# Down products in another order: high products of four chunks first, the sixth product's last chunks by bank pairs, and four tiles' norms in common stages

## The chip, the cores and the metric

The kernel runs on one core of a Trainium2 chip. The metric is device time in microseconds of one execution; smaller is better. All outputs are float32.

## The reference

One layer of a streaming encoder over 1024 tokens of width 1024: a half feed-forward block (FFN 1), a mixer of two attentions, and a second half feed-forward block (FFN 2). What the change touches is the second matrix product of each feed-forward block and the norm that follows:

```python
def rms_norm(x, g):
    x32 = x.astype(jnp.float32)
    y = x32 * lax.rsqrt(jnp.mean(x32 * x32, axis=-1, keepdims=True) + EPS)
    return (y * g.astype(jnp.float32)).astype(x.dtype)

def swiglu(u, w_gate, w_up, w_down):
    return (jax.nn.silu(u @ w_gate) * (u @ w_up)) @ w_down

def sublayer(h, i, fn, resid_w):
    ...
    u = rms_norm(h, norm_pre[l, i]) * (1.0 + scale) + shift
    return h + resid_w * gate * rms_norm(fn(u), norm_post[l, i])

h = sublayer(h, 0, lambda u: swiglu(u, ffn1_w_gate[l], ffn1_w_up[l], ffn1_w_down[l]), 0.5)
h = sublayer(h, 1, ..., 1.0)
h = sublayer(h, 2, lambda u: swiglu(u, ffn2_w_gate[l], ffn2_w_up[l], ffn2_w_down[l]), 0.5)
```

The product with `w_down` is 1024 tokens by 2816 by 1024.

## The kernel before

**Numbers.** A float32 product is made of three passes. Each operand is split into a high part (a rounded copy, made by ScalarE, `ACT.copy`) and a low part (the rest, made by VectorE, `tensor_sub`); TensorE adds high x high, high x low and low x high. In the down stage one 128 x 512 piece of an operand comes from DRAM into a staging tile `stg`, and `halves` (lines 217 and 218) makes `sbH`, `sbL` (activations, the stationary side) or `tbH`, `tbL` (weights, the moving side) of it.

**Seven products.** Each big matrix product is done by a scheme with seven half-size products in place of eight (Strassen's, in Winograd's form): sums and differences of the quarters of both matrices are made beforehand and lie in DRAM (`hd`, `d_S`, `d_T`). In the down stage (`ffn`, from line 558) the loop over `p` runs the seven products. The first six have 11 chunks `c` of 128 along the inner dimension; a chunk has four token tiles `m` with a PSUM bank each, and three matmuls of 128x128 by 128x512 a bank (`mm`, lines 578 to 582): 132 matmuls a product. Products use bank set A or B in turns; sixth and seventh both use A. The seventh (`p == 6`) goes over the chunks twice, in `h = 0` for banks 0 and 1 and in `h = 1` for banks 2 and 3, with 256 columns of `sb` each time.

**Buffers.** There are six staging tiles (`STG = 6`), that is, three chunks' worth; six buffers each of `sbH` and `sbL` (`SB = 6`), and eleven each of `tbH` and `tbL`. A staging tile is free again when both the cast on ACT and the subtraction on DVE have read it, and only then can the load of a later piece be issued on the queue of the SP engine.

**After a product** VectorE or ScalarE adds or copies the banks into the eight token tiles `y` (lines 643 to 656). The first four tiles are complete after the fifth product (`p == 4`, line 653); the others after the seventh. The sixth product's sums are read out of the banks at line 656 (`y[4 + m] += bank[m]`); the seventh product adds on in the same banks, so its first matmul into a bank waits for that line's read of the bank.

**Norms.** `finish(t)` loads a residual tile (`res`, two buffers in FFN 1, seven in FFN 2), and `post_norm_tile` takes the sum of squares on ACT (`Square` with accumulation), a `Sqrt` on ACT, a reciprocal, a scalar-tensor-tensor and an addition on DVE, and the store. In FFN 1 `pre_norm` follows for the next sublayer: again a square, a root and a reciprocal, and a multiplication (line 164). The norms of the four first tiles are called one after another after the fifth product.

**Order.** Work is written in the order shown; a scheduler places the instructions on each engine's queue, and every queue is then served strictly in its order. The code around the down stage (`hidden` for the last chunk pair, on DVE) directly precedes the first product.

Of the kernel before, what the change touches and what calls it, by code (L numbers as in the profile page):

```python
# [12 lines left out]
F32 = mybir.dt.float32  # L13
F32R = mybir.dt.float32r
BF16 = mybir.dt.bfloat16
AF = mybir.ActivationFunctionType
ALU = mybir.AluOpType
# [3 lines left out]
P = 128  # L21
# [25 lines left out]
def build(ctx, tc, A, out):  # L47
# [148 lines left out]
    def wproj(ps, w, half):  # L196

        H, L = w
        mm3(ps, [((H[:, k * P:(k + 1) * P], L[:, k * P:(k + 1) * P]), U[k, half]) for k in range(NK)])

    def post_norm_tile(y, g, res, dst, parts=1, tail=False):

# [297 lines left out]
    def ffn(wg, wu, wd, start, pending, steps_fn, per_pair, steps2_fn, i, res_src, dst):  # L500
# [57 lines left out]
        open_y()  # L558
        with tc.tile_pool(name="ffb0", bufs=1, side="left", reuse_waits="tile") as np_, \
                tc.tile_pool(name="ffb", bufs=1, side="left", reuse_waits="tile") as fp, \  # L560
                tc.tile_pool(name="ffb_ps", bufs=4, space=PSUM, reuse_waits="tile") as psum:
            grow = np_.tile([P, D], F32, name="grow", tag="grow")
            if i == 2:
# [11 lines left out]
                loads.append(SP.dma_start(t, A[wd][c][:, B[n]] if n in B else hd[n, c]))  # L575
                return t

            def mm(ps, s, t, ts, first, last, check):
                (sH, sL), (tH, tL) = s, t
                PE.matmul(ps, sH[:, ts], tH, start=first, stop=False, skip_group_check=not check)  # L580
                PE.matmul(ps, sH[:, ts], tL, start=False, stop=False, skip_group_check=not check)  # L581
                PE.matmul(ps, sL[:, ts], tH, start=False, stop=last, skip_group_check=not check)  # L582

            copies = []
            y = [y_tile(t) for t in range(NT)]
# [3 lines left out]
            def finish(t):  # L589
# [4 lines left out]
                if i + 1 in ab:  # L594
                    pre_norm(y[t])

            for p, (sn, tn, bk) in enumerate((("A11", "B11", "A"), ("A12", "B21", "B"), ("S2", "T2", "A"), ("S1", "T1", "B"),
                                              ("S4", "B22", "B"), ("S3", "T3", "A"), ("A22", "T4", "A"))):
                if p in (0, 1, 3):
# [3 lines left out]
                bank = banks[bk]  # L603
                fresh = p in (0, 1, 3)
                if p < 6:
                    for c in range(NPAIR):
                        ahead = ExitStack()
                        if p == 4 and c >= 3:

                            for ins in copies:  # L610
                                ahead.enter_context(tc.issue_after(ins))
                        with ahead:
                            s, t = halves(fp, raw(sn, c), "sb", SB), halves(fp, raw(tn, c), "tb", NPAIR)
                        if c in STEPS[p]:
                            next(steps, None)
                        for m in range(4):
                            mm(bank[m], s, t, slice(m * P, (m + 1) * P), fresh and c == 0, c == NPAIR - 1, fresh)
                else:
                    ts = []
                    turned = iter(())  # L620
# [2 lines left out]
                    for h in range(2):  # L623
                        for c in range(NPAIR):
                            if h == 0 and c == 0:
                                next(steps, None)
                            with ExitStack() as ahead:
                                if h == 0 and c >= 3:
                                    for ins in copies:
                                        ahead.enter_context(tc.issue_after(ins))  # L630
                                r = raw(sn, c)
                                s = halves(fp, r[:, h * 256:(h + 1) * 256], "sb", SB, 256)
                                if h == 0:
                                    ts.append(halves(fp, raw(tn, c), "tb", NPAIR))
# [8 lines left out]
                for m in range(4):  # L643
# [7 lines left out]
                        copies.append((V.tensor_copy if m % 2 else ACT.copy)(y[4 + m][:, d1], bank[m]).ins)  # L651
                    elif p == 4:
                        V.tensor_add(y[m][:, d1], bank[m], y[m][:, d1])
                        finish(m)
                    elif p == 5:
                        copies.append(V.tensor_add(y[4 + m][:, d1], bank[m], y[4 + m][:, d1]).ins)  # L656
                if p == 6:
# [739 lines left out]
```

## Time and profile before

| | us |
|---|---|
| median of 3 runs (2235.43 to 2240.99) | 2236.72 |
| profiled execution | 2242.12 |
| its span, first to last instruction | 2240.4 |
| DVE busy | 1552.1 |
| ACT busy | 1050.0 |
| down stage of FFN 1, first matmul | 486.87 |
| fifth product of FFN 1 ends about | 642.8 |
| down stage of FFN 2, first matmul | 2013.84 |
| last matmul of FFN 2 about | 2228.9 |

The profile's page gives the engines' busy time and the groups of instructions; the trace behind it gives every instruction's start, the idle time before it in brackets with what ended it, and windows in which busy time, instruction count and the granted clock of TensorE are summed. PE is TensorE, DVE is VectorE, ACT is ScalarE, SPq is the queue on which DMAs are issued. A matmul's shown length is longer than the distance to the next one, since matmuls are pipelined.

### The profile page before, as it was taken

How to read it: one execution, taken by the hardware profiler on the slowest of the kernel's cores; microseconds unless marked ns; L12 is line 12 of the kernel's file. 1: busy time of each engine (PE TensorE's matmuls, PEld its weight loads, DVE VectorE, ACT ScalarE, POOL GpSimd, SP SyncE). 2: the span in 40 equal slices, each digit the busy share in tenths (PEclk: the TensorE clock that was granted, in tenths of full speed). 3: DMA queues.
4: the chain of work that ended last, by engine and by line, in shares of the span. 5: the costliest groups of instructions: out<-in, count | busy, mean ns of one | idle time of the engine just before them, and what ended most of it. 6: DMA issues, size and time to landing. Idle time of an engine off the chain costs nothing.

```text
span 2240.4 us, 28449 instructions
## 1 busy us (share of the span) xinstructions
PE 2155.7 (96%) x10328; PEld 1780.0 (79%) x10328; DVE 1552.1 (69%) x2646; ACT 1050.0 (47%) x1893; POOL 61.5 (3%) x84
## 2 busy tenths in 40 slices
PE   6999999999998999999999999999999999999997
PEld 4777788878887877888888988788877788878886
DVE  7979767567577688576677676665985766655566
ACT  6633324235456556455455454565733333334454
POOL 0000000000000011001011000000000000000000
PEclk9999999999999999999999999999999999999999
DMA  8488635359785111110211123653474544538666
GB/s 327 146 281 280 211 130 185 127 183 328 245 291 201 50 45 46 33 54 26 70 55 64 36 94 100 236 202 128 148 239 166 184 173 144 179 111 277 215 224 213
DMA packets 139792, 361.27 MB, mean 161 GB/s; under 512 B 19458, under 2 KB 23682, under 8 KB 139651
## 3 DMA queue, kind: packets, MB, share of 16 engines
q1 hardware_dynamic: 138018, 353.68, 46.4%
q0 software_dynamic: 1632, 5.77, 0.7%
q8 instruction: 81, 1.33, 0.2%
q14 instruction: 61, 0.49, 0.1%
HBM read 270.77 MB, written 88.62 MB: 160 GB/s over the span
## 4 chain that ended last, share of the span: by engine, by line
PE 68%; DVE 19%; DMA 6%; ACT 4%; issue 3%; SPq 0%; DVEq 0%; ACTq 0%
PE bank L295 8%; PE bank L293 7%; PE bank L294 7%; PE pps L841 4%; PE pps L843 4%; PE pps L845 4%; PE bankA L581 3%; PE bankA L582 3%; PE bankA L580 3%; PE bankB L580 3%; PE bankB L582 3%; PE bankB L581 3%; DVE f L1050 2%; DVE wsL L218 2%; DMA wada<-in_wada 2%
## 5 line engine op out<-in xcount | busy, mean ns | idle before, releaser
L841 PE MATMUL pps<-uH,wsH 128*128 128x512 f32 x512 | 209.0, 408 | 0.0
L843 PE MATMUL pps<-uL,wsH 128*128 128x512 f32 x512 | 203.8, 398 | 0.0
L845 PE MATMUL pps<-uH,wsL 128*128 128x512 f32 x512 | 203.2, 397 | 0.0
L218 DVE TENSOR_TENSOR tbL<-stg,tbH 128x512 fp32r<-128x512 f32 x154 | 105.9, 689 | 97.9 <-ACT tbH L217 97.6
L217 ACT CAST tbH<-stg 128x512 fp32r<-128x512 f32 x154 | 95.6, 621 | 141.9 <-DMA stg<-d_T 98.8
L581 PE MATMUL bankA<-tbL,sbH 128*128 128x512 f32 x352 | 139.8, 397 | 6.3 <-DVE tbL L218 6.3
L580 PE MATMUL bankA<-tbH,sbH 128*128 128x512 f32 x352 | 140.1, 398 | 5.5 <-DVE y L656 5.1
L293 PE MATMUL bank<-uH,wsH 128*128 128x512 f32 x352 | 139.1, 401 | 4.1 <-ACT wsH L217 3.5
L294 PE MATMUL bank<-uL,wsH 128*128 128x512 f32 x352 | 140.2, 398 | 1.6 <-DVE uL L748 1.5
L582 PE MATMUL bankA<-tbH,sbL 128*128 128x512 f32 x352 | 139.6, 396 | 0.7 <-DVE sbL L218 0.7
L295 PE MATMUL bank<-uH,wsL 128*128 128x512 f32 x352 | 139.5, 397 | 0.6 <-DVE wsL L218 0.6
L134 DVE TENSOR_TENSOR wsL<-raw,wsH 128x1024 fp32r<-128x1024 f32 x72 | 88.0, 1222 | 68.1 <-ACT wsH L133 67.6
L217 ACT CAST wsH<-s 128x1024 fp32r<-128x1024 f32 x88 | 92.2, 1049 | 85.8 <-DVE s L327 69.8
L217 ACT CAST sbH<-stg 128x512 fp32r<-128x512 f32 (+1 forms) x176 | 98.3, 565 | 62.7 <-DMA stg<-hd_A 47.4
L218 DVE TENSOR_TENSOR sbL<-stg,sbH 128x512 fp32r<-128x512 f32 (+1 forms) x176 | 108.5, 620 | 27.0 <-ACT sbH L217 26.1
L360 ACT COPY q<-bank 128x512 f32<-128x512 f32 x44 | 25.5, 588 | 193.1 <-PE bank L295 193.1
L845 PEld LDWEIGHTS pps<-uH,wsL 128*128 128x128 f32 x512 | 96.6, 189 | 17.7
L218 DVE TENSOR_TENSOR wsL<-s,wsH 128x1024 fp32r<-128x1024 f32 x88 | 107.0, 1217 | 3.5 <-ACT wsH L217 3.2
L841 PEld LDWEIGHTS pps<-uH,wsH 128*128 128x128 f32 x512 | 97.3, 190 | 14.5
L843 PEld LDWEIGHTS pps<-uL,wsH 128*128 128x128 f32 x512 | 97.0, 189 | 14.3
L217 ACT CAST wsH<-raw 128x1024 fp32r<-128x1024 f32 (+1 forms) x88 | 73.3, 834 | 74.0 <-PE bank L294 49.8
L580 PE MATMUL bankB<-tbH,sbH 128*128 128x512 f32 x264 | 102.7, 389 | 0.0
(246 smaller groups left out, 5905.7 us busy)
## 6 DMA issues: line engine op xcount, KB each, us to landing
wada<-in_wada SPq DMA_DIRECT2D x56, 512.0 KB, 5.7
raw<-in_wg SPq DMA_DIRECT2D x50, 512.0 KB, 6.5
raw<-in_wu SPq DMA_DIRECT2D x50, 512.0 KB, 4.6
raw<-in_wd SPq DMA_DIRECT2D x44, 512.0 KB, 4.3
stg<-hd_A SPq DMA_DIRECT2D x88, 256.0 KB, 4.5
stg<-d_S SPq DMA_DIRECT2D x88, 256.0 KB, 3.5
stg<-d_T SPq DMA_DIRECT2D x88, 256.0 KB, 3.9
d_S<-s SPq DMA_DIRECT2D x40, 512.0 KB, 2.7
```

The costliest lines, as they stand in the source:

```text
L134: eng.tensor_sub(l, raw, h.bitcast(F32))
L217: ACT.copy(h, src)
L218: eng.tensor_sub(l, src, h.bitcast(F32))
L293: PE.matmul(ps, H[:, ks], bH, start=first and k == 0, stop=False, skip_group_check=not first)
L294: PE.matmul(ps, H[:, ks], bL, start=False, stop=False, skip_group_check=not first)
L295: PE.matmul(ps, L[:, ks], bH, start=False, stop=k == 3, skip_group_check=not first)
L580: PE.matmul(ps, sH[:, ts], tH, start=first, stop=False, skip_group_check=not check)
L581: PE.matmul(ps, sH[:, ts], tL, start=False, stop=False, skip_group_check=not check)
L582: PE.matmul(ps, sL[:, ts], tH, start=False, stop=last, skip_group_check=not check)
L841: PE.matmul(ps, aH, bH, start=i == 0, stop=False)
L843: PE.matmul(ps, aH, bL, start=False, stop=False)
L845: PE.matmul(ps, aL, bH, start=False, stop=i == n - 1)
```

## The change

Three edits, all in the down stage of both feed-forward blocks.

1. In the first product the high x high matmuls of chunks 0 to 3 (16 of them) are issued first, and then the other two passes of the four chunks (32).
2. In the sixth product the last three chunks are done for banks 0 and 1, and then for banks 2 and 3.
3. The norms of the tiles 0 to 3 are no longer four chains. `rstd4` takes the squares of four tiles into four columns, and one root and one reciprocal serve all four; `finish4` does the rest tile by tile. It is a generator that the sixth product advances by one step a chunk, and the seventh too (`due`).

```diff
+    def rstd4(pool, srcs):
+        ss = pool.tile([P, 4], F32, name="ss4", tag="ss4", bufs=2)
+        for n, src in enumerate(srcs):
+            junk = mpool.tile([P, D + 64], BF16, name="junk", tag="junk", bufs=1)
+            ACT.activation(junk[:, :D], src, AF.Square, scale=1.0 / 32.0, accum_out=ss[:, n:n + 1])
+            yield
+        sq = pool.tile([P, 4], F32, name="sq4", tag="sq4", bufs=2)
+        ACT.activation(sq, ss, AF.Sqrt, bias=eps)
+        r = pool.tile([P, 4], F32, name="rs4", tag="rs4", bufs=2)
+        V.reciprocal(r, sq)
+        return r
...
-            def mm(ps, s, t, ts, first, last, check):
+            def mm(ps, s, t, ts, first, last, check, part=(0, 1, 2)):
                 (sH, sL), (tH, tL) = s, t
-                PE.matmul(ps, sH[:, ts], tH, start=first, stop=False, skip_group_check=not check)
-                PE.matmul(ps, sH[:, ts], tL, start=False, stop=False, skip_group_check=not check)
-                PE.matmul(ps, sL[:, ts], tH, start=False, stop=last, skip_group_check=not check)
+                for n, (a, b) in enumerate(((sH, tH), (sH, tL), (sL, tH))):
+                    if n in part:
+                        PE.matmul(ps, a[:, ts], b, start=first and n == 0, stop=last and n == 2, skip_group_check=not check)
...
+            def finish4():
+                r = yield from rstd4(nrm, [y[t] for t in range(4)])
+                yield
+                for t in range(4):
+                    res = np_.tile([P, D], F32, name="res", tag="res", bufs=res_bufs)
+                    SP.dma_start(res, res_src(t))
+                    V.scalar_tensor_tensor(y[t], y[t], r[:, t:t + 1], grow, ALU.mult, ALU.mult)
+                    V.tensor_add(y[t], y[t], res)
+                    SP.dma_start(dst(t), y[t])
+                    yield
+                if i + 1 in ab:
+                    r = yield from rstd4(nrm, [y[t] for t in range(4)])
+                    yield
+                    for t in range(4):
+                        V.tensor_scalar_mul(y[t], y[t], r[:, t:t + 1])
+                        yield
...
-                        for m in range(4):
-                            mm(bank[m], s, t, slice(m * P, (m + 1) * P), fresh and c == 0, c == NPAIR - 1, fresh)
+                        if p == 5:
+                            next(due, None)
+
+                        def block(c, s, t, ms=range(4), **kw):
+                            for m in ms:
+                                mm(bank[m], s, t, slice(m * P, (m + 1) * P), fresh and c == 0, c == NPAIR - 1, fresh, **kw)
+
+                        if p == 0 and c < 4:
+                            block(c, s, t, part=(0,))
+                            held.append((c, s, t))
+                            if c == 3:
+                                for x in held:
+                                    block(*x, part=(1, 2))
+                        elif p == 5 and c >= NPAIR - 3:
+                            block(c, s, t, (0, 1))
+                            held.append((c, s, t))
+                            if c == NPAIR - 1:
+                                for x in held:
+                                    block(*x, (2, 3))
+                        else:
+                            block(c, s, t)
...
+                            if h == 0:
+                                next(due, None)
+                            else:
+                                for _ in due:
+                                    pass
...
                         V.tensor_add(y[m][:, d1], bank[m], y[m][:, d1])
-                        finish(m)
+                        if m == 3:
+                            due = finish4()
```

**TensorE at the start of FFN 1's down stage.** The names carry buffer numbers: before, chunk 0 has `tbH_3809`, `tbL_3810`, `sbH_3803` and `sbL_3804`; banks are `bankA_3797` to `bankA_3800`. Before:

```order
L295 MATMUL bank_3635<-T4H_723,wsL_3682 128x512
L580 MATMUL bankA_3797<-tbH_3809,sbH_3803 128x512
L581 MATMUL bankA_3797<-tbL_3810,sbH_3803 128x512
L582 MATMUL bankA_3797<-tbH_3809,sbL_3804 128x512
L580 MATMUL bankA_3798<-tbH_3809,sbH_3803 128x512
L581 MATMUL bankA_3798<-tbL_3810,sbH_3803 128x512
```

In the changed kernel (its line 596 is the matmul; chunk 0 has 3806 to 3813, chunk 2 `tbH_3844`, chunk 3 `tbH_3860`; banks 3800 to 3803), from the end of chunk 2's high products on:

```order
L596 MATMUL bankA_3802<-tbH_3844,sbH_3838 128x512
L596 MATMUL bankA_3803<-tbH_3844,sbH_3838 128x512
L596 MATMUL bankA_3800<-tbH_3860,sbH_3854 128x512
L596 MATMUL bankA_3801<-tbH_3860,sbH_3854 128x512
L596 MATMUL bankA_3802<-tbH_3860,sbH_3854 128x512
L596 MATMUL bankA_3803<-tbH_3860,sbH_3854 128x512
L596 MATMUL bankA_3800<-tbL_3813,sbH_3806 128x512
L596 MATMUL bankA_3800<-tbH_3812,sbL_3807 128x512
```

Chunk 3's four high products now stand ahead of every matmul that uses a low part.

**VectorE where FFN 1's sixth product ends.** Before, the last stretch of the four chains of norms (tiles `y0` to `y3`) stands ahead of the four reads of the banks (line 656); `sbL` and `tbL` of size 256 and 512 are operands of the seventh product.

```order
L149 RECIPROCAL rs_5258<-sq_5256 128x1
L149 RECIPROCAL rs_5269<-sq_5267 128x1
L206 SCALAR_TENSOR_TENSOR y3_3792<-y3_3792,rs_5269,grow_3788 128x1024
L164 TENSOR_SCALAR y2_3791<-y2_3791,rs_5258 128x1024
L208 TENSOR_TENSOR y3_3792<-y3_3792,res_5262 128x1024
L656 TENSOR_TENSOR y4_3793<-bankA_3797,y4_3793 128x512
```

In the changed kernel (line 211 is the reciprocal, 619 the addition of the residual, 626 the multiplication, 716 the read of a bank, 231 the subtraction):

```order
L619 TENSOR_TENSOR y2_3794<-y2_3794,res_5408 128x1024
L619 TENSOR_TENSOR y3_3795<-y3_3795,res_5437 128x1024
L231 TENSOR_TENSOR sbL_5516<-stg_5513,sbH_5515 128x256
L231 TENSOR_TENSOR tbL_5522<-stg_5519,tbH_5521 128x512
L231 TENSOR_TENSOR sbL_5536<-stg_5533,sbH_5535 128x256
L211 RECIPROCAL rs4_5553<-sq4_5551 128x4
L626 TENSOR_SCALAR y0_3792<-y0_3792,rs4_5553 128x1024
L626 TENSOR_SCALAR y1_3793<-y1_3793,rs4_5553 128x1024
L626 TENSOR_SCALAR y2_3794<-y2_3794,rs4_5553 128x1024
L716 TENSOR_TENSOR y4_3796<-bankA_3800,y4_3796 128x512
L716 TENSOR_TENSOR y5_3797<-bankA_3801,y5_3797 128x512
L231 TENSOR_TENSOR tbL_5542<-stg_5539,tbH_5541 128x512
```

The reads of banks 0 and 1 now stand behind the second common reciprocal and three multiplications; the reads of banks 2 and 3 stand five rows further down.

More of the change, by code (lines that the diff above doesn't have):

```diff
@@ L560, in ffn @@
                 tc.tile_pool(name="ffb", bufs=1, side="left", reuse_waits="tile") as fp, \
+                tc.tile_pool(name="nrm", bufs=1, side="left", reuse_waits="tile") as nrm, \
                 tc.tile_pool(name="ffb_ps", bufs=4, space=PSUM, reuse_waits="tile") as psum:
@@ L595, in finish @@
                     pre_norm(y[t])
+            def finish4():
[14 more added lines that the diff above has]
+                        yield
+            due = iter(())
             for p, (sn, tn, bk) in enumerate((("A11", "B11", "A"), ("A12", "B21", "B"), ("S2", "T2", "A"), ("S1", "T1", "B"),
@@ L605, in ffn @@
                 if p < 6:
+                    held = []
                     for c in range(NPAIR):
```

## Prediction

> **What bounds the kernel now.** I read the page's busy shares first, then the waits of TensorE over the two down stages (FFN 1 from 478 to 740 us, FFN 2 from 1990 us to the end), then TensorE's windows and the timeline around the two largest waits.
>
> ```profile
> PE 2155.7 (96%) x10328; PEld 1780.0 (79%) x10328; DVE 1552.1 (69%) x2646; ACT 1050.0 (47%) x1893; POOL 61.5 (3%) x84
> PE bankA L580 <- DVE y L656: 5.1, 1, 5.1
> PE bankA L581 <- DVE tbL L218: 3.0, 1, 3.0
> PE bankA L581 <- DVE tbL L218: 3.3, 2, 3.0
> ```
>
> TensorE is the bound. The second and third rows are FFN 1's, the last FFN 2's: two waits of 3.0 us at the start of the first product, one of 5.1 us between sixth and seventh product in FFN 1, and none there in FFN 2. The change touches these places. No instruction of weight is added or taken away, so everything turns on TensorE's idle time and its clock. The windows (time, PE busy and count, granted clock, DMA share, GB/s) price both:
>
> ```profile
> 486.87:496.39 9.52, 6.49 (x16) 0.65 0.77 256
> 2013.84:2023.11 9.27, 6.24 (x21) 0.82 0.75 248
> 672.37:681.38 9.01, 3.88 (x11) 0.81 0.78 263
> 681.38:694.30 12.92, 12.92 (x58) 1.00 0.86 291
> ```
>
> A warm matmul takes 12.92 / 57 gaps = 0.2267 us. The first three windows are the three places; the counts hold one matmul of the product before or of the window's edge. What is lost is the window less its matmuls at 0.2267: 15 of the product's own between 486.87 and 496.43 lose 9.56 - 15 x 0.2267 = 6.16 us; 19 between 2013.84 and 2023.11 lose 9.27 - 4.31 = 4.96 us; ten from 672.37 to 681.38 lose 9.01 - 2.27 = 6.74 us. So each stall costs more than its wait, and the rest is the clock (here each row also has PEld, DVE, ACT and POOL before the clock):
>
> ```profile
> 489.56:492.98 3.42, 2.69 (x6) 2.16 (x7) 3.08 (x6) 0.00 (x0) 0.30 (x1) 0.51 0.99 320
> 492.98:496.39 3.41, 3.41 (x9) 2.65 (x8) 0.85 (x2) 1.25 (x3) 0.00 (x0) 0.50 1.02 338
> 496.39:499.80 3.41, 3.41 (x16) 2.79 (x15) 3.23 (x6) 2.99 (x5) 0.00 (x0) 0.99 1.03 306
> 677.30:680.71 3.41, 2.82 (x7) 2.27 (x8) 3.41 (x8) 1.62 (x4) 0.00 (x0) 0.51 0.81 275
> ```
>
> The clock is granted in steps of 3.41 us. At 0.50 a step has 8 gaps between its 9 matmuls, at 0.99 it has 15 between 16: 47% of a cold step is lost, 1.6 us. A step that was 79% busy (2.69 of 3.42) was followed by a cold one, a step 83% busy (2.82) by a warm one. A restart was cold for 2.9 us at least (677.9 to 680.8) and 6.1 us at most (490.3 to 496.4): 1.36 to 2.88 us.
>
> **Part 1, high products of four chunks first.** FFN 1's timeline:
>
> ```profile
> 484.56 0.61 ACT L217 CAST tbH<-stg 128x512 fp32r<-128x512 f32 x1
> 486.87 0.39 PE L580 MATMUL bankA<-tbH,sbH 128*128 128x512 f32 x1
> 488.94 0.69 DVE L218 TENSOR_TENSOR sbL<-stg,sbH 128x512 fp32r<-128x512 f32 x1
> 489.66 0.33 SPq L575 DMA_DIRECT2D stg<-hd_A  x1
> 490.26 0.33 SPq L575 DMA_DIRECT2D stg<-in_wd  x1
> 490.29 0.80 PE L581 MATMUL bankA<-tbL,sbH 128*128 128x512 f32 x1 [3.03 <-DVE tbL L218]
> 494.89 0.62 ACT L217 CAST sbH<-stg 128x512 fp32r<-128x512 f32 x1 [9.71 <-DMA stg<-hd_A]
> 495.42 0.61 ACT L217 CAST tbH<-stg 128x512 fp32r<-128x512 f32 x1
> ```
>
> TensorE begins at 486.87 and needs the first low part at once; VectorE is still busy with the stage before and makes its first, `sbL`, at 488.94. The 16 high products would be 16 x 0.2267 = 3.6 us of work for a wait of 3.0. But only six staging tiles exist, three chunks' worth: their casts end at 484.56 + 0.61, and then ACT sits idle for 9.71 us. Chunk 3's pieces need tiles that VectorE has first to read: the load is issued at 489.66, 0.03 us after `sbL` is made, and its weights' cast ends at 495.42 + 0.61 = 496.03. In the change chunk 3's four high products stand ahead of all low products in TensorE's queue, so 32 low products whose operands are ready from 490 us on stand behind them. The wait moves from the low part of chunk 0 to the high part of chunk 3. SP's and VectorE's orders at this place are as before, so I take 496.08 for the restart (0.05 us from the cast's end to the matmul), with 12 matmuls done: 9.21 - 12 x 0.2267 = 6.49 us lost, and the cold restart (the idle time fills more than one step) between 1.36 and 2.88; I take the middle, 2.1, since where in a step it restarts is open. 8.6 against 6.16: **+2.4 us** (+1.7 to +3.2).
>
> ```profile
> 2013.84 0.39 PE L580 MATMUL bankA<-tbH,sbH 128*128 128x512 f32 x1
> 2016.63 0.33 SPq L575 DMA_DIRECT2D stg<-hd_A  x1
> 2022.60 0.62 ACT L217 CAST tbH<-stg 128x512 fp32r<-128x512 f32 x1
> ```
>
> FFN 2 is alike: first matmul 2013.84, chunk 3's load issued 2016.63, its weights cast by 2023.22, restart at 2023.26 or 2023.27. 9.42 - 12 x 0.2267 = 6.70 us, and 2.1 for the clock: 8.8 against 4.96, **+3.8 us** (+3.1 to +4.6). Before, TensorE used the gap for chunks 0 and 1 at half clock; in the change it cannot.
>
> The Trainium skill ("TensorE: Matmul & The Clock Gate", "Part 1: The HAM clock gate", under "What's actually happening") says that TensorE falls to half clock after at least one idle window of about 3.4 us, and is at full clock again after one busy one. The trace agrees on the second (492.98 to 496.39 is full, and the next step stands at 0.99) but not on the first: a stall of 3.03 us already made the next step cold. By that page each restart pays one cold window, 1.6 us: the two places would come to +1.9 and +3.3 in place of +2.4 and +3.8, an estimate, and the sum below to 1.0 us less. Its rule speaks against gathering idle time into one gap as well.
>
> **Parts 2 and 3, FFN 1.** The timeline around the wait of 5.1 us:
>
> ```profile
> 645.52 2.48 DVE L653 TENSOR_TENSOR y<-bankB,y 128x512 f32<-128x512 f32 x4
> 646.48 1.05 ACT L143 ACTIVATE junk<-y 128x1024 bf16<-128x1024 f32 x1
> 648.16 1.28 ACT L147 ACT_TABLE_LOAD   x1
> 673.87 0.16 DVE L149 RECIPROCAL rs<-sq 128x1 f32<-128x1 f32 x1 [1.23 <-ACT sq L147]
> 677.07 1.88 DVE L656 TENSOR_TENSOR y<-bankA,y 128x512 f32<-128x512 f32 x3
> 677.89 0.76 PE L580 MATMUL bankA<-tbH,sbH 128*128 128x512 f32 x1 [5.13 <-DVE y L656]
> 679.86 0.68 DVE L218 TENSOR_TENSOR tbL<-stg,tbH 128x512 fp32r<-128x512 f32 x1
> 680.60 0.32 SPq L575 DMA_DIRECT2D stg<-d_T  x1
> 691.85 0.69 DVE L218 TENSOR_TENSOR tbL<-stg,tbH 128x512 fp32r<-128x512 f32 x1 [0.21 <-ACT tbH L217]
> ```
>
> The seventh product's first matmul may only start once VectorE has read the bank at line 656, and that stands behind the fourth chain of norms: the last reciprocal at 673.87 waits for ACT. What the chains cost, by the groups (busy time, mean ns, idle before) and the residual's loads:
>
> ```profile
> L206 DVE SCALAR_TENSOR_TENSOR y<-y,rs,grow 128x1024 f32<-128x1024 f32 (+1 forms) x26 | 31.0, 1200 | 0.6
> L208 DVE TENSOR_TENSOR y<-y,res 128x1024 f32<-128x1024 f32 (+1 forms) x26 | 29.4, 1138 | 0.1
> L164 DVE TENSOR_SCALAR y<-y,rs 128x1024 f32<-128x1024 f32 x20 | 15.4, 768 | 1.6 <-DMA h_dram<-y 1.5
> DMA to landing us min/median/max: 3.9/4.9/6.2
> ```
>
> The change by hand. The sums are ready at 648.0; four squares of 1.05 us between casts, and the table load of 1.28, put the common root at about 654.4. Reciprocal, two scalings and two additions (2 x 1.20 + 2 x 1.14) end at 659.3; two more scalings with the subtractions of chunks 8 to 10 between them at 665.3, in time for the sixth product's last chunk. The residuals of tiles 2 and 3 stand on SP behind the stores of tiles 0 and 1, issued about 660, and land about 4.9 us later, 665 to 666.5; the additions end at 667.7, the second squares and root at 670.0, the reciprocal and three multiplications (0.67 each) at 672.7, and the reads of banks 0 and 1 (0.62 each) at 673.9. TensorE, ready at 672.37 + 0.23 = 672.6, starts about 673.9 in place of 677.9: 4.0 us earlier.
>
> Not all of it is kept. The seventh product's later loads are released by VectorE three chunks back, in a loop that starts with the first low parts after line 656. The change puts a low part between the reads of banks 0, 1 and 2, 3, so line 656's last read ends at about 677.4 by hand, against 679.6 (just ahead of `tbL` at 679.86): the loop moves by 2.2 us. Before, chunk 10's `tbL` ended at 692.54, about 0.6 us before TensorE used it. TensorE can gain 2.2 + 0.6 = **2.8 us**, and I take that; the bounds are 6.7 (the whole loss) and nothing. Bank pairs alone cost nothing: the last 36 matmuls are the same, and VectorE gets banks 0 and 1 earlier than it can use them, behind the norms.
>
> **Parts 2 and 3, FFN 2.**
>
> ```profile
> 2191.13 0.37 SPq L575 DMA_DIRECT2D stg<-d_T  x1
> 2196.50 2.73 DVE L656 TENSOR_TENSOR y<-bankA,y 128x512 f32<-128x512 f32 x4 [0.74 <-PE bankA L582]
> 2212.46 0.69 DVE L218 TENSOR_TENSOR tbL<-stg,tbH 128x512 fp32r<-128x512 f32 x1 [2.11 <-ACT tbH L217]
> 2212.48 0.50 PE L580 MATMUL bankA<-tbH,sbH 128*128 128x512 f32 x1 [0.38 <-ACT tbH L217]
> ```
>
> Here line 656 waits for TensorE and there is no stall to win. The common root makes the stores of tiles 2 and 3 later, and the seventh product's loads of chunks 1 and 2 (2191.13 is the issue of chunk 1's weights) stand on SP behind the last of them, about 2.8 us later than before by a hand sum like the one above. The start at 2198.8 is still met, but chunks 6 to 10, of which chunk 10 already waits 0.38 us, come about 1 us later. I take **+0.3 us**; bounds -0.7 (the small waits gone) and +2.5 (the delay in full). The fewer roots and reciprocals (about 0.3 and 0.16 us each) run on ACT and VectorE beside TensorE and give nothing; were VectorE the bound there, they would give 6 x 0.16 = 1.0 us.
>
> **Sum.** +2.4 + 3.8 - 2.8 + 0.3 = +3.7 us. The profiled execution took 2242.12 (span 2240.4, 1.7 around it) and would take 2245.8; it lies 5.4 above the median of the runs, 2236.72, which becomes **2240.4**. A measurement of this kernel can tell 0.3% from no change, 6.7 us: below 2230.0 is faster, above 2243.4 slower.
>
> **The rivals.**
> - *The stall only lengthens* (forecast, 0.60): 2240.4, with the terms' bounds of the likely size about 2234 to 2247.
> - *The change does what it says* (0.07): the high products cover VectorE's lateness and the seventh product starts early. First products -6.16 and -4.96, the middle -6.7: 2218.9, or 2222 with part of the clock lost. For it: 3.6 us of matmuls against 3.0 us of wait. Against: chunk 3 has no staging tile before 489.66, and its load to cast took over 5 us. It needs that load to be issued some 5 us earlier.
> - *One wait for another* (0.10): restart and clock happen to equal those of before (the shortest wake and a cast 1 us earlier), the seventh product gains: -2.8 + 0.3, 2234.2.
> - *Slower* (0.23): the seventh product's supply. If line 656's last read and with it the load now at 680.60 do not come earlier, TensorE starts early but waits for the loop at its end, and the middle gives nothing. It decides once VectorE's common norms (two residuals behind two stores on SP, 6.2 us at worst) end 2.2 us later than my hand sum. With the longest cold restart in both first products, +3.2 + 4.6 + 0 + 0.9 = +8.7: 2245.4.
>
> **How the numbers follow.** Forecast and "one wait for another" lie mostly within 0.3% (0.54 + 0.08), the forecast's upper end reaches 2247, and "slower" has its price just beyond the limit (most of its 0.23). Together: faster 0.09, the same 0.64, slower 0.27. The range for 8 in 10 reaches from 2232, which takes in the one-for-one case, to 2247, the sum of the dear ends.
>
> **What will show it.** Right: at both starts one wait of TensorE of 5 to 7 us on ACT's `tbH`, at chunk 3's first high product, in place of 3.0 us on `tbL`, with at most 12 matmuls before it and a clock near 0.5 behind it; at FFN 1's seventh product a wait of 1 to 2 us on the bank's read in place of 5.1, and new waits on `tbL` or `tbH` around chunks 9 and 10. Wrong: chunk 3's cast ended before about 490, no wait at the start, or a wait on the bank's read as long as before. If the start of FFN 2 gains while FFN 1's loses, the cause is not the staging tiles.

## The result: slower by 0.56%

The changed kernel takes 2252.61 us (median of 6 runs, 2247.13 to 2256.30), the kernel before 2238.56 (6 runs, 2235.43 to 2240.99): a ratio of 1.0056, with a 95% interval of 1.0045 to 1.0067, or 10 to 15 us more. The forecast was 2240.4 with a range of 2232 to 2247, so the time lies outside it.

TensorE's waits in the two down stages of the changed kernel (engine, tile, line, what it waited for; sum in us, times, longest). The first five rows are FFN 1's, the others FFN 2's:

```profile
PE bankA L596 <- ACT tbH L230: 7.3, 4, 4.9
PE bankA L596 <- DVE sbL L231: 2.1, 3, 1.7
PE bankA L596 <- DVE y L716: 1.6, 1, 1.6
PE bankA L596 <- DVE q L363: 1.1, 1, 1.1
PE bankA L596 <- DVE tbL L231: 0.9, 4, 0.2
PE bankA L596 <- ACT tbH L230: 5.6, 1, 5.6
PE bankA L596 <- DVE q L363: 0.6, 1, 0.6
PE bankA L596 <- DVE tbL L231: 0.2, 1, 0.2
```

Both waits of 3.0 us on `tbL` at the start are gone, and a wait of 4.9 or 5.6 us on ScalarE's `tbH` stands in their place. The wait on the bank's read before FFN 1's seventh product fell from 5.1 to 1.6 us, as the change meant it to. But there are new, shorter waits on `tbH`, `tbL` and `sbL`, and they are in the seventh product. The timeline shows the first product's start, and the windows (time, PE busy and count, clock, DMA share, GB/s) what followed:

```profile
486.29 0.39 PE L596 MATMUL bankA<-tbH,sbH 128*128 128x512 f32 x1
487.78 2.80 PE L596 MATMUL bankA<-tbH,sbH 128*128 128x512 f32 x11 [1.10 <-DVE q L363]
495.53 2.07 PE L596 MATMUL bankA<-tbH,sbH 128*128 128x512 f32 x4 [4.95 <-ACT tbH L230]
```

```profile
495.48:499.88 4.40, 4.35 (x11) 0.51 0.86 258
2033.05:2038.80 5.75, 5.75 (x14) 0.50 0.90 312
676.20:698.22 22.02, 18.71 (x66) 0.92 0.89 302
```

Twelve high products, the wait for chunk 3, and then 4.4 us (FFN 1) and 5.8 us (FFN 2) at half clock. The third window is the first half of the seventh product, the pass `h = 0` with its 66 matmuls: 22.02 us. Before, the same pass took 16.42 (the row also counts the next pass's first matmul):

```profile
677.89:694.31 16.42, 16.42 (x67) 0.91 0.88 298
```

A table of stretches tells where the time went. Each is the distance between the first matmuls of two products in the trace; 132 warm matmuls are 132 x 0.2267 = 29.92 us, and four products 119.7.

| us, one profiled execution each | before | changed | difference |
|---|---|---|---|
| up to FFN 1's down stage | 486.87 | 486.29 | -0.6 |
| FFN 1, first product | 36.13 | 38.53 | +2.4 |
| FFN 1, second to fifth | 119.68 | 119.68 | 0.0 |
| FFN 1, sixth and seventh | 71.33 | 75.46 | +4.1 |
| between the two down stages | 1299.83 | 1303.64 | +3.8 |
| FFN 2, first product | 34.90 | 39.62 | +4.7 |
| FFN 2, second to fifth | 119.68 | 119.68 | 0.0 |
| FFN 2, from the sixth to the end | 71.93 | 71.60 | -0.3 |
| span | 2240.4 | 2254.5 | +14.1 |

The forecast had +2.4, -2.8, +3.8 and +0.3 for the first product, the sixth and seventh, FFN 2's first product and its end. The second of them has the wrong sign and is off by 6.9 us. The 3.8 us between the stages lie in unchanged code. The two profiled executions, 2242.12 and 2256.30 us, lie 3.6 and 3.7 above their medians, so their difference is nearly that of the medians.

### The profile page after: what moved, and what is told of

Same layout as the page of the kernel before. It is cut to its first block, busy times and chain, and to the rows that moved or that the text cites. A ratio compares the mean times of both kernels' runs of the same rounds, so it can differ in the third digit from the quotient of the medians.

```text
span 2254.5 us, 28448 instructions
## 1 busy us (share of the span) xinstructions
PE 2161.8 (96%) x10328; PEld 1781.3 (79%) x10328; DVE 1551.3 (69%) x2637; ACT 1049.8 (47%) x1884; POOL 61.6 (3%) x84
## 4 chain that ended last, share of the span: by engine, by line
PE 61%; DVE 21%; DMA 9%; ACT 5%; issue 4%; SPq 0%; DVEq 0%; ACTq 0%
PE bank L308 8%; PE bank L306 7%; PE bank L307 7%; PE bankA L596 6%; PE bankB L596 5%; PE pps L901 4%; PE pps L903 4%; PE pps L905 4%; DVE f L1110 2%; DVE wsL L231 2%; DMA stg<-d_T 2%; DMA wada<-in_wada 2%; DVE q L363 1%; PE vps L901 1%; PE vps L905 1%
```

## The experiments

Each kernel was timed against the kernel before on the same chip; ratios are this to before, with 95% intervals. "Issue" is how long after the sixth product's first matmul the seventh product's first weights load was issued in FFN 1. The times of products come from one profiled execution of each kernel; it lies within 4.6 us of the kernel's median, but for rest_only's, which took 2257.12 us, the most of its twelve runs and 13.2 us above their median.

| run | median, us | ratio | FFN 1 first | FFN 1 6th + 7th | issue | between | FFN 2 first | FFN 2 1st to 5th |
|---|---|---|---|---|---|---|---|---|
| before | | | 36.13 | 71.33 | 13.7 | 1299.8 | 34.90 | 154.6 |
| before_again | 2243.29 | | 34.79 | 74.29 | 16.5 | 1298.6 | 33.28 | 154.8 |
| changed | 2252.61 | 1.0056 (1.0045 to 1.0067) | 38.53 | 75.46 | 19.9 | 1303.6 | 39.62 | 159.3 |
| highs4_only | 2248.70 | 1.0039 (1.0025 to 1.0054) | 38.23 | 73.53 | 14.9 | 1297.3 | 38.65 | 158.3 |
| rest_only | 2243.91 | 1.0024 (1.0010 to 1.0037) | 34.88 | 76.96 | 20.7 | 1303.4 | 33.28 | 155.6 |
| highs3_only | 2238.32 | 0.9994 (0.9985 to 1.0003) | 32.50 | 73.04 | 15.0 | 1295.2 | 32.02 | 155.7 |
| norms_only | 2245.88 | 1.0030 (1.0018 to 1.0041) | 34.81 | 73.08 | 19.4 | 1297.2 | 34.85 | 154.5 |
| pairs_only | 2243.43 | 1.0012 (1.0001 to 1.0023) | 34.74 | 72.12 | 13.6 | 1297.8 | 34.86 | 156.5 |
| highs4_stg8 | 2237.82 | 0.9987 (0.9975 to 0.9999) | 31.33 | 73.79 | | 1299.0 | 30.90 | 154.4 |
| after_stg8 | 2235.36 | 0.9973 (0.9959 to 0.9986) | 31.33 | 69.68 | 10.7 | 1299.6 | 30.86 | 152.3 |
| highs3_reads_first | 2240.99 | 0.9998 (0.9987 to 1.0009) | 32.63 | 72.65 | | 1295.3 | 32.28 | 155.2 |
| rest_spread | 2243.78 | 1.0013 (1.0003 to 1.0022) | 34.83 | 74.00 | 17.7 | 1297.2 | 34.87 | 154.6 |
| rest_stg8 | 2239.76 | 0.9997 (0.9987 to 1.0006) | 34.84 | 70.03 | 12.6 | 1297.0 | 34.87 | 154.6 |
| before_stg8 | 2241.33 | 1.0000 (0.9991 to 1.0010) | 34.83 | 72.21 | 13.5 | 1298.9 | 34.86 | 155.2 |
| highs3_res4 | 2247.35 | 1.0027 (1.0018 to 1.0037) | 32.08 | 73.59 | | 1307.1 | 36.46 | 156.2 |
| after_stg8_res4 | 2243.49 | 1.0015 (1.0003 to 1.0026) | 31.33 | 71.34 | | 1304.7 | 35.50 | 155.2 |
| highs3_res4pad | 2238.35 | 0.9987 (0.9977 to 0.9998) | 32.40 | 70.72 | | 1299.0 | 31.89 | 152.7 |
| after_stg8_res4pad | 2232.07 | 0.9962 (0.9948 to 0.9977) | 31.31 | 69.89 | | 1297.1 | 30.85 | 151.1 |

### Which part costs what

**highs4_only**, part 1 alone:

```diff
-                        elif p == 5 and c >= NPAIR - 3:
+                        elif False:
...
-                        if m == 3:
-                            due = finish4()
+                        finish(m)
```

> Only part 1 (high products of four chunks first); sixth product and norms as before. Theory 'staging tiles': chunk 3 cannot be staged, so both first products lengthen as in the changed kernel, by 2.4 us (FFN 1) and 4.7 us (FFN 2), and everything else stays: +7.1 us against before. Rival 'drift': the 3.7 us that the changed kernel's unchanged middle (between the two feed-forward blocks) showed follow from part 1 as well: about +11 us. Rival 'the norms alone': the first products would cost nothing without the other parts: 0 us.

**rest_only**, parts 2 and 3 alone:

```diff
-                        if p == 0 and c < 4:
+                        if False:
```

> Only parts 2 and 3 (bank pairs, common norms); first product as before. Theory: FFN 1's sixth and seventh product together are 4.1 us longer as in the changed kernel, FFN 2's 0.4 shorter: +3.7 us against before. Rival 'drift' (the unchanged middle's 3.7 us belong to this part): about +7.5 us. Rival 'interplay': the seventh product only starves because the first product was late: 0 to -2.8 us, the predicted gain.

**norms_only** (both edits to the order of matmuls undone) and **pairs_only** (the first edit of rest_only and the last of highs4_only):

> Only part 3 (norms in common stages), without the bank pairs and with the first product as before. If the common stages alone starve the seventh product (theory), +3 to +5 us in FFN 1's sixth and seventh product together, as with the pairs. If the bank pairs are the cause, 0 to -2.8 us.

> Part 2 alone (last three chunks of the sixth product by bank pairs), norms in single chains. The reads of the banks stand behind the norms on VectorE as before, so theory says no change: within 0.3% of before, FFN 1's sixth and seventh product 71 to 74 us, wait 5 to 7 us. If the pairs are what made 77.0 us of 73.1 (the two runs with common norms), 75 us or more.

Part 1 alone costs 0.39%, or 8.7 us, parts 2 and 3 together 0.24%, 5.4 us; the sum, 14.1 us, agrees with what the whole costs. An interplay of the parts isn't seen; the intervals are some 6 us wide, so a small one isn't ruled out, and they hold the sums expected by theory as well as those of "drift". The stretch between the down stages speaks against drift from part 1: 1297.3 us in highs4_only, less than before. The norms alone cost about as much as both together (0.30%, the intervals overlap), and the bank pairs alone show 0.12%, with an interval that all but touches nothing, and the sixth and seventh product as before: the pairs aren't needed for the loss, though a share of up to 5 us isn't excluded.

Where in the kernel the norms cost this is less clear. Rest_only's profile shows 77.0 us for the sixth and seventh product, but in an execution that doesn't stand for its median. Norms_only's profile, 1.6 us above that of before, shows 73.1 us, where 3 to 5 us more than before was expected; that is within the scatter of single chains (before_again, below).

**before_again** is the kernel before, profiled a second time.

> The kernel before, a second profile, to see how much a stretch of unchanged code differs between two executions. The two kernels with part 1 alone had the same sixth and seventh product as before, yet FFN 1's took 73.0 and 73.5 us against 71.3, with waits of 6.2 and 6.5 us in place of 5.1. If that is chance, this profile lies between 71 and 74 us, and the middle between the two down stages between 1295 and 1304 us. If it comes from part 1, this one repeats 71.3 and 5.1.

```profile
PE bankA L580 <- DVE y L656: 7.3, 1, 7.3
PE bankA L581 <- DVE tbL L218: 3.0, 1, 3.0
```

The sixth and seventh product took 74.3 us here, just above the 71 to 74 that chance was given. The wait before the seventh product was 7.3 us, and 4.1 to 7.3 us over all runs with the chains of norms as before. The profile from which the forecast was made had 5.1 and 71.33 us for the sixth and seventh product; all seven profiles with six tiles and the chains as before lie between 70.7 and 74.3, with a mean of 72.7. The stretch between the down stages ran from 1295.2 to 1303.6 us, leaving aside the two runs in which the start of the next stage waited longer.

### Part 1: the staging tiles

Both have part 1 without the others, as highs4_only has. **highs3_only** holds three chunks in place of four, **highs4_stg8** keeps four and gives them tiles:

```diff
-                        if p == 0 and c < 4:
+                        if p == 0 and c < 3:
...
-                            if c == 3:
+                            if c == 2:
```

```diff
-STG = 6
-SB = 6
+STG = 8
+SB = 5
```

> Part 1 with three chunks held in place of four, which is what six staging tiles hold; the rest as before. Theory 'staging tiles': after 12 high products the first low part is there, 24 low products of about 5.4 us bridge until chunk 3 is cast: no wait over 1.5 us at the start and no cold clock, FFN 1's first product 4.5 to 5 us shorter than before, FFN 2's about 4 us: -8 to -9 us. Rival 'VectorE is late anyway': the low parts of chunks 1 and 2 come too late, the wait only moves: -2 to +2 us.

> Part 1 alone with four chunks held, and eight staging tiles in place of six (five buffers of sbH and sbL in place of six make the room). Theory 'staging tiles': chunk 3 can be loaded with the others, its cast no longer waits for VectorE, the wait of 5.0 to 5.8 us on tbH goes, and the first products take about 32 us each in place of 38.2 and 38.7. Rival 'issue' (SP or ACT are late with chunk 3 whatever the tiles): they stay at 38 us.

With three chunks, and with four chunks and eight tiles, the wait on `tbH` in FFN 1's first product is gone. The waits of highs4_only (two rows), and then those of highs4_stg8, in that product:

```profile
PE bankA L596 <- ACT tbH L230: 5.0, 1, 5.0
PE bankA L596 <- DVE q L363: 1.1, 1, 1.1
```

```profile
PE bankA L596 <- DVE q L363: 1.1, 1, 1.1
```

The first products fell to 31.3 and 32.5 us (FFN 1) and 30.9 and 32.0 (FFN 2), with no matmul at half clock: the fourth chunk's staging tiles are the cause of the lengthened first products, shown by both. But the total fell by 0.06% and 0.13% only, 1.3 and 2.9 us, the first within its interval of nothing, where 8 to 9 were expected. FFN 1's first product alone is 2.3 and 3.5 us shorter than the 34.8 us that most executions of the old order took. In FFN 2 what the first product won was lost in the next ones: the first to fifth took 155.7 and 154.4 us, about as before (154.6). Highs3_only's waits there:

```profile
PE bankA L596 <- ACT sbH L230: 0.8, 1, 0.8
PE bankA L596 <- DVE q L363: 0.6, 1, 0.6
PE bankB L596 <- ACT y L710: 0.6, 1, 0.6
PE bankA L596 <- ACT tbH L230: 0.3, 1, 0.3
PE bankA L596 <- DVE tbL L231: 0.2, 1, 0.2
```

Only `sbH` and `y`, 1.4 us, lie in the second to fifth product, which took 123.6 us in place of 119.7. The rest are matmuls in these products that start 0.3 to 0.5 us after the one before in place of 0.23, which this view doesn't count, at a clock of 1.00.

### Why FFN 2 gives the gain back

Seven residual loads of 512 KB stand on SP's queue among the loads of FFN 2's second and third product. **highs3_res4** and **after_stg8_res4** load four there:

```diff
-                res_bufs = 2 + 5
+                res_bufs = 4
```

> Part 1 with three chunks, and four residual buffers in FFN 2 in place of seven. In all kernels so far FFN 2's first to fifth product together took at least 152 us and, where the first was shorter, the later ones were longer by as much (32.0 + 123.6, 32.3 + 122.9, 33.3 + 122.3, 34.9 + 119.7). Theory: the seven residual loads of 512 KB that stand among the loads of the second and third product slow the supply, and TensorE waits for it once it is early. With three of them moved behind the stores of the norms, the later four products come back to 120 to 121 us: first to fifth 152 to 153 us in place of 155.6, total about 3 us below the run with three chunks. Rival 'the staging tiles' round trip' (three chunks in flight are too few whatever else moves): 155 us stay.

> The changed kernel with eight staging tiles and four residual buffers in FFN 2. If the residual loads are what gives the gain back, first to fifth product of FFN 2 take 150 to 151 us in place of 152.3 and the total lies about 1.5 us below the run with eight tiles; if the round trip is, nothing changes. Against before: 0.997 or below.

Neither told it. FFN 2's first matmul waited 5.4 and 6.6 us on ACT's first `tbH`, more waits followed, and both kernels were slower than with seven. By the order of the pools in the kernel, a smaller one puts the staging tiles elsewhere in the on-chip memory. **highs3_res4pad** and **after_stg8_res4pad** keep the room:

```diff
+                np_.tile([P, 3 * D], F32, name="pad", tag="pad")
```

> As the run with three chunks and four residual buffers, but the room of the three buffers is kept by an unused tile, so that the staging tiles lie at the addresses they had with seven (without it they moved, and the first loads of FFN 2's down stage waited 5.4 us more). First product of FFN 2 32 us again. Theory 'residual loads': first to fifth product 152 to 153 us. Rival 'round trip of the staging tiles': 155 to 156 us.

> The changed kernel with eight staging tiles and four residual buffers in FFN 2, room kept as above. Theory 'residual loads': first product 30.9 us again, first to fifth 150 to 151 us. Rival 'round trip': 152 us as with seven. Total against before: 0.997 or below by both.

With the room kept the waits on the first `tbH` are gone, so the lost room was their cause and not the fewer loads; the trace doesn't show what the first loads waited for. Now the first products are as short as without the edit, and the first five together fall from 155.7 to 152.7 us, as the theory of the residual loads said, and from 152.3 to 151.1. The six-tile kernels with seven loads lie between 154.5 and 156.5 (the changed kernel and highs4_only aside), so the first fall is clear of the scatter and the second is not. In the totals no gain is shown: highs3_res4pad's interval overlaps with highs3_only's, and after_stg8_res4pad's with after_stg8's. All waits over those five products in highs3_res4pad:

```profile
PE bankA L597 <- DVE q L363: 0.6, 1, 0.6
PE bankB L597 <- ACT y L711: 0.4, 1, 0.4
PE bankA L597 <- ACT tbH L230: 0.2, 1, 0.2
PE bankA L597 <- DVE tbL L231: 0.2, 1, 0.2
```

### Parts 2 and 3: the seventh product's head start

In `h = 0` a chunk is six matmuls, 6 x 0.2267 = 1.36 us, and needs 512 KB; at the 302 GB/s of that window this is 1.7 us (an estimate from the two). TensorE outruns the loads there and lives on what is staged beforehand. Before, the cast of chunk 5's weights began at 676.57 and the product at 677.89: the weights of six chunks were cast by then. In the changed kernel the product began at 676.20, and the cast of chunk 2's weights at 676.51: two. VectorE's timeline and SP's queue of the changed kernel show why:

```profile
656.99 0.18 DVE L211 RECIPROCAL rs<-sq 128x4 f32<-128x4 f32 x1 [0.92 <-ACT sq L209]
657.20 2.48 DVE L618 SCALAR_TENSOR_TENSOR y<-y,rs,grow 128x1024 f32<-128x1024 f32 x2
659.60 2.35 DVE L619 TENSOR_TENSOR y<-y,res 128x1024 f32<-128x1024 f32 x2
661.87 1.27 DVE L618 SCALAR_TENSOR_TENSOR y<-y,rs,grow 128x1024 f32<-128x1024 f32 x1
663.07 0.68 DVE L231 TENSOR_TENSOR sbL<-stg,sbH 128x512 fp32r<-128x512 f32 x1
```

```profile
656.10 0.32 SPq L589 DMA_DIRECT2D stg<-d_T  x1
660.85 1.45 SPq L620 DMA_DIRECT2D h_dram<-y  x2
662.35 1.41 SPq L617 DMA_DIRECT2D res<-in_x  x2
663.86 0.43 SPq L589 DMA_DIRECT2D stg<-hd_A  x1
664.39 0.38 SPq L589 DMA_DIRECT2D stg<-d_T  x1
```

The common reciprocal is followed by five operations in one piece. From 657.2 to 663.1 VectorE reads no staging tile, none comes free, and SP issues no load for a product between 656.1 and 663.9; two stores and two residual loads that wait for the same additions stand there too. The seventh product's first weights are asked for at 664.39, 19.9 us after the sixth product's start, where it was 13.7 (656.37). Windows of that piece in the changed kernel and of the same piece before (time, then PE, PEld, DVE, ACT and POOL busy, clock, DMA share, GB/s):

```profile
657.00:663.00 6.00, 6.00 (x28) 4.99 (x27) 5.96 (x6) 4.76 (x8) 0.00 (x0) 1.00 0.46 179
```

```profile
655.20:661.20 6.00, 6.00 (x28) 4.99 (x27) 4.07 (x8) 3.03 (x8) 0.00 (x0) 1.00 0.97 314
```

The DMA engines were half idle, 0.46 against 0.97. The missing transfers are made up later, when the seventh product needs its own: around its start a load took 5.2 us at the median to land, before 3.7 (from 674 to 694 us, and 672 to 692):

```profile
DMA to landing us min/median/max: 2.7/5.2/6.1
```

```profile
DMA to landing us min/median/max: 2.6/3.7/5.4
```

**after_stg8**, **rest_stg8** and **before_stg8** have eight staging tiles (the edit of highs4_stg8) in the whole change, in parts 2 and 3, and in the kernel before:

> The changed kernel whole, with eight staging tiles in place of six (five buffers of sbH and sbL). First products as in the run with part 1 alone and eight tiles, about 32 us each. For the seventh product: theory 'lost head start' (before, six chunks of the seventh product are loaded and cast when it starts, in the changed kernel three, and its first half uses a chunk every 1.36 us, faster than one can be loaded): one chunk more of head start, its waits on tbH and tbL (3.3 us in sum) at most half, FFN 1's sixth and seventh product 72 to 74 us in place of 75.5. Rival 'bytes' (transfers of stores and residuals take the bandwidth): waits and 75 us stay.

> Parts 2 and 3 with eight staging tiles (five buffers of sbH and sbL), the first product as before. If the head start decides, FFN 1's sixth and seventh product take 69 to 71 us as with the whole change and eight tiles (69.7), and the first products stay at 33 to 36 us each: 1 to 3 us above the whole change with eight tiles, below before. If part 1 has a hand in it, 73 us or more.

> The kernel before with eight staging tiles (five buffers of sbH and sbL), nothing else changed: what the tiles give alone. The wait before the seventh product hangs on the norms, not on loads: it stays at 5 to 7 us and FFN 1's sixth and seventh product at 71 to 74 us; the first products stay at 33 to 36 us. Within 0.3% of before (theory). If the tiles alone are the gain, 2235 as in the changed kernel with eight tiles.

With eight tiles the common norms give what was hoped of them: 69.7 and 70.0 us for the sixth and seventh product, against 72.2 and 73.8 with single chains and eight tiles, and 73.1 to 77.0 in the four profiles with common norms and six (rest_spread, below, is one). The two later kernels with common norms and eight tiles have 69.9 and 71.3. After_stg8's waits in the two products:

```profile
PE bankA L596 <- DVE sbL L231: 1.8, 1, 1.8
PE bankA L596 <- DVE y L716: 0.5, 1, 0.5
PE bankA L596 <- DVE tbL L231: 0.4, 2, 0.2
```

Nothing is left on `tbH`. Yet the block is still there, as SP's queue of after_stg8 shows, and loads around the seventh product's start (666 to 686 us) take as long to land as in the changed kernel:

```profile
648.55 0.32 SPq L589 DMA_DIRECT2D stg<-d_T  x1
653.30 1.46 SPq L620 DMA_DIRECT2D h_dram<-y  x2
654.81 1.40 SPq L617 DMA_DIRECT2D res<-in_x  x2
656.30 0.44 SPq L589 DMA_DIRECT2D stg<-hd_A  x1
```

```profile
DMA to landing us min/median/max: 3.1/5.3/6.9
```

The seventh product's first weights are asked for 10.7 and 12.6 us after the sixth product's start, but the second chunk's only at 19.0 and 20.9, behind the block. At the product's start the weights of three chunks are cast in both, one more than in the changed kernel and half of what there was before. What the two tiles change most is how closely the loads follow: the sixth chunk's weights are cast 3.9 us after the product's start in after_stg8, and 8.0 us after it in the changed kernel. By these traces it is the supply during the first pass that decides, and the six chunks of head start are one way to have it.

That the tiles alone give nothing is shown by before_stg8 (1.0000). The tiles turn the changed kernel from 0.56% slower to 0.27% faster than before. Its bytes are the same, so the rival "bytes" falls. Rest_stg8's total stays at before's (0.9997) where below was expected: the 2 to 3 us that it wins in the stretch are about the width of its interval.

**rest_spread** has parts 2 and 3, with each tile's scaling and addition held back behind the subtractions of a chunk:

```diff
                 r = yield from rstd4(nrm, [y[t] for t in range(4)])
                 yield
+                yield
+                yield
                 for t in range(4):
...
+                    with tc.issue_after(subs[-1]):
                         V.scalar_tensor_tensor(y[t], y[t], r[:, t:t + 1], grow, ALU.mult, ALU.mult)
                         V.tensor_add(y[t], y[t], res)
```

(`subs` holds the subtractions of `halves`; the store stands in the same block.)

> Parts 2 and 3 as in the run with these two alone, but each tile's scaling and addition wait for the subtractions of chunks 7, 8, 9 and 10 of the sixth product, so that VectorE no longer does four of them (4.8 us) in one piece without freeing a staging tile. If that block is what takes the seventh product's head start, its first weights load is issued about 3 to 5 us earlier in the sixth product than the 19.4 to 19.9 us after the product's start that the common norms showed (13.7 and 15.0 us with single chains), and FFN 1's sixth and seventh product take 72 to 74 us in place of 77.0. If not (the stores and residuals ahead of the loads on SP decide, or the pairs), 75 to 77 us stay.

The load was issued at 17.7 us, 2 to 3 earlier than with the block and not 3 to 5, and the stretch came to 74.0, between norms_only's 73.1 and rest_only's 77.0; the total's interval overlaps with rest_only's. This agrees with the block as a part of it, but doesn't show it. The stores and residual loads, which still stood ahead of the next loads on SP, may be another part; no run took them away.

**highs3_reads_first** is highs3_only with the rest of the last tile's norm, and the second norms of tiles 2 and 3, put behind the four reads of the banks, between the seventh product's subtractions. The main piece of its edit:

```diff
+            def last_tile(r3):
+                res = np_.tile([P, D], F32, name="res", tag="res", bufs=res_bufs)
+                SP.dma_start(res, res_src(3))
+                for c in range(4):
+                    yield
+                V.scalar_tensor_tensor(y[3], y[3], r3, grow, ALU.mult, ALU.mult)
+                yield
+                V.tensor_add(y[3], y[3], res)
+                SP.dma_start(dst(3), y[3])
+                yield
+                if i + 1 in ab:
+                    pre_norm(y[2])
+                    yield
+                    pre_norm(y[3])
```

> Part 1 with three chunks; norms in single chains as before, but the rest of tile 3's norm and tile 2's second norm stand behind the four reads of the banks that the seventh product waits for, between its subtractions. If the head start of six chunks is what matters, and it is kept here, the wait before the seventh product falls from 5 to 6 us to under 2 and FFN 1's sixth and seventh product take 67 to 69 us: about 4 us below the run with three chunks alone, 2233 to 2235. Rival 'the seventh product is bound by its loads anyway': the gain at its start is given back in waits on tbH and tbL, 71 to 73 us.

The rival was right. The wait at the start fell to 1.8 us, and the stretch stayed at 72.7 us: what the earlier start gave was lost again in waits on `tbH`, `tbL` and `sbL`. With six tiles the seventh product is bound by its loads here, and an earlier start without earlier loads was worth nothing that the profile shows.

## Why the prediction was wrong

- **First product, the mechanism: right.** The wait moved to chunk 3's first high product, with twelve matmuls done. The restart came 9.24 us after the first matmul in FFN 1 (495.53 - 486.29) where 9.21 was worked out, and 9.45 in FFN 2 where it was 9.42. The loss, first product less 29.92, was 8.6 us in FFN 1 (forecast 8.6) and 9.7 in FFN 2 (forecast 8.8; 8.7 in highs4_only).
- **What it was compared with: mis-sized.** The 6.16 us of loss before were one execution's, with 13 matmuls at half clock. Seven other executions of the same start lost 4.8 to 5.0 us (34.74 to 34.88), so part 1 costs FFN 1 about 3.5 us and not 2.4. For FFN 2 it is 3.8 and 4.7 us (38.65 and 39.62 against 34.9), within the forecast's bounds or just above. And the base of the forecast, the median of three runs, lay 1.8 us below that of all six.
- **FFN 2's first product as a term of its own: half right.** A longer one costs in full (the second to fifth took 119.7 us as before). A shorter one gave nothing in highs3_only and highs4_stg8 and about half of itself in after_stg8 (152.3 us for the first to fifth against 154.6). The forecast needed only the first half.
- **Sixth and seventh product, "-2.8": the step that failed**, and the sign with it. The start was worked out well (673.9; it came at 676.20, of which 1.8 is the later start of the sixth product). The step behind it was not: "in a loop that starts with the first low parts after line 656". The loop starts in the sixth product: before, the first low part of the seventh product's weights was made 14 us ahead of its first matmul, and the weights of six chunks were cast when it began. The hand sum put the block of scalings and additions in order and asked only whether the sixth product's last chunk was in time. It was. What the block kept from being freed, the staging tiles of the next product, wasn't asked; in the changed kernel's profile it left two of the six chunks. The stretch came to 75.5 us, and to 73.1 to 77.0 in the other three profiles with common norms and six tiles, where 68.5 (71.3 - 2.8) was forecast. In total, parts 2 and 3 cost 5.4 us (2.2 to 8.3) where a gain of 2.5 was forecast. The sign named for the forecast, a wait of 1 to 2 us on the bank's read, did appear (1.6); the waits on `tbH` and `tbL` behind it, expected around chunks 9 and 10, began at chunk 3 and came to 3.3 us.
- **The rival "slower"** named the right place, the seventh product's supply, and priced it at no gain where it was a loss: 2.8 us in the changed kernel's stretch against the mean of 72.7.
- **FFN 2's sixth and seventh product, "+0.3"**: -0.3 in the profile, within its bounds. The kernel before itself had 71.0 and 71.9 us in its two profiles, so one profile can't tell.
- **The clock.** Restarts ran at half clock for 4.4 and 5.8 us, inside the 2.9 to 6.1 taken as bounds. The Trainium skill ("TensorE: Matmul & The Clock Gate", "Part 1: The HAM clock gate") gives a restart one window of about 3.4 us. By that rule the first products would have cost 1.0 us less than forecast; they cost as much in FFN 1 and 0.9 us more in FFN 2.
- **Left open.** First products (about 3.5 + 4) and sixth and seventh (about 3) make some 10.5 us of the measured 10 to 15. The profile also shows 3.8 us more between the down stages, in unchanged code. Rest_only's long execution shows the same, norms_only and rest_spread do not, and the other kernels scatter from 1295 to 1300. Whether a part of it belongs to the change was not settled, nor where the norms' cost lies in norms_only, whose profile shows next to none of it.

## What to carry to other kernels

When operations are gathered into one block on an engine that also frees buffers, follow the buffers and not only the result: here the price fell due a product later, at the place that eats staged work faster than it can be loaded, and a deeper ring of staging tiles took it away without removing the block. Work that is pulled forward to cover a wait can reach only as far as the buffers do; a chunk more than they hold turns the cover into a longer wait. And a stretch should be priced from more than one execution where a single wait varies by 3 us, as the one before the seventh product did.

Of the kernels run, the changed one with eight staging tiles, five `sb` buffers, four residual buffers in FFN 2 and the room of the others kept was the fastest: 2232.07 us, 0.9962 of before (0.9948 to 0.9977).

## What the runs showed of the hardware that was not expected

- The same wait of 3.02 to 3.03 us at FFN 2's start slowed the clock in six executions that had it (34.85 to 34.90 us for the product) and didn't in two, before_again and rest_only (33.28 us). Before_again's window over that wait, whose clock stayed at 1.00:

```profile
2015.78:2022.60 6.82, 3.79 (x17) 1.00 0.65 214
```

- A pool made smaller by three buffers, which by the kernel's order moves the next pool in memory, made the first matmul of a stage wait 5.4 and 6.6 us longer; an unused tile of the same size took this back. Why the first loads came later there, no trace shows.
